# A one-core decoder layer on Trainium2: small tiles padded so that matmul operands start at the same place modulo 256 bytes

## The chip, the cores and the metric

The kernel runs on 1 core of one Trainium2 chip. The metric is the time of one execution in microseconds (us), as the device reports it; the figure used is the median of several runs. For the kernel before the change it is 2510.06 us (3 runs, 2508.91 to 2510.13).

## What is computed

One layer of a decoder trunk over 2048 tokens of width 1024, all in float32, with normalisation before and after each half. The first half mixes tokens by two head groups, a chunkwise mLSTM (4 heads) and a causal attention with compressed keys and values (8 heads); the second half is a feed-forward network of width 4096 with a squared ReLU.

```python
a = rmsnorm(x, norm_pre_mix[l])
mix = token_mixer(a, cos, sin, w_in[l], ...)   # [mLSTM || attention](a @ w_in) @ w_out
x = x + rmsnorm(mix, norm_post_mix[l])
m = rmsnorm(x, norm_pre_mlp[l])
y = jnp.square(jax.nn.relu(m @ w_up[l])) @ w_down[l]
x = x + rmsnorm(y, norm_post_mlp[l])
```

## The kernel before

Every large product is made of TensorE matmuls of fp32r tiles in three passes: each float32 operand is split into a high part, rounded to fp32r, and the rest, the low part, and the kernel adds high by high, high by low and low by high (the helper `mm3`, lines 198 to 200, and the same three lines written out in `up`, lines 2107 to 2109, and in `down`, 2339 to 2341). Nearly every one of these matmuls has 128 stationary columns (512 bytes of each partition) and 512 moving columns (2048 bytes of each partition). The splits are made by ScalarE (the high part, a cast) and VectorE or GpSimd (the subtraction).

The work has five stages; the times are of the profiled execution.

1. Input projection and mLSTM, 0 to about 490 us: `unit` (line 400) and `values` (832) multiply the weights `wh`, `wl` by the transposed input `xh`, `xl`; `chunk` (878) runs the recurrence.
2. Attention, to about 1040 us: `maxima` (1384) and `step` (1444) make scores `S` from `Kh`, `Kl` and `Qh`, `Ql`, then multiply the exponentials `ph`, `pl` by the values `V` (lines 1483 and 1486). `V` is one tile whose slices lie 129 numbers (516 bytes) apart.
3. Output projection, to about 1205 us: `group` (1714) multiplies `wo` by `hh`, `hl`, k tile by k tile (eight of them).
4. Up product, to about 1790 us: `up` (2092) makes seven products for each pair of column blocks (a Strassen scheme), 12 matmuls each.
5. Down product, to the end: `down` (2326), the same scheme with 6 matmuls a product, adds into the tiles `y` (`into`, line 2350), and `finish` (2399) normalises and stores.

The order on each engine is found beforehand by a small planner (`Plan`, with costs and due times given by hand) and then pinned. Transfers are issued by the SP queue in the planner's order.

SBUF tiles come from pools that are stacked from the left end and from the right end of each partition's bytes, a pool at a time (`sb`, line 202). A tile takes its bytes rounded up to a multiple of 32. Nearly all tiles are multiples of 256 bytes, so where a pool's tiles start modulo 256 is set by the few small ones that were placed before them: `mhalf` (line 228, 32 bytes), `col` (140 bytes), the row maxima `mx` (16 bytes, line 1423), the sums `rsm` (16 bytes, line 1570), `onecol` (260 bytes, line 1163), `gcol` (32 bytes, line 1678) and `v2` (64 bytes, line 2231).

Of the kernel before, what the change touches and what calls it, by code (L numbers as in the profile page):

```python
# [10 lines left out]
F32 = mybir.dt.float32  # L11
F32R = mybir.dt.float32r
# [6 lines left out]
P = 128  # L19
SEQ = 2048  # L20
DM = 1024
KD = DM // P
TB = 512
NB = SEQ // TB
NT = SEQ // P
# [164 lines left out]
def trunk(ctx: ExitStack, tc: tile.TileContext, x, xT, pos, wu, uqw, ukw, uvw, wout, wup, wdn, cols, rows, consts, edge, out, dbg=None):  # L190
# [3 lines left out]
    vec, act, pool, pe = nc.vector, nc.scalar, nc.gpsimd, nc.tensor  # L194
# [7 lines left out]
    def sb(stack, name, bufs, side="left"):  # L202
        return stack.enter_context(tc.tile_pool(name=name, bufs=bufs, side=side, reuse_waits="tile"))
# [17 lines left out]
    top = ctx.enter_context(tc.tile_pool(name="top", bufs=1))  # L221
# [3 lines left out]
    col = top.tile([P, C_N], F32, tag="col", name="col")  # L225
    ident = cst[:, K_ID : K_ID + P]
    maskT = cst[:, K_MASKT : K_MASKT + P]
    mhalf = top.tile([P, 8], F32, tag="mhalf", name="mhalf")
    identr = top.tile([P, P], F32R, tag="identr", name="identr")

    hT = dram.tile([DM, SEQ], F32, tag="hT", name="hT")
# [11 lines left out]
    pl = Plan()  # L243
    mark = len(nc.cur_bb.bb.instructions)
    s_b, s_x, s_e, pc, pa = (ExitStack() for _ in range(5))
    b1 = sb(s_b, "b1", 1, "right")
    b2 = sb(s_b, "b2", 2, "right")
    ps1 = pp(s_b, "ps1", 1, "right")
# [900 lines left out]
    def switch3():  # L1149

        nonlocal av, ar2, pS, po, V, maskb, identb, onecol
        s_b.close()
        av = sb(pa, "av", 1, "right")
        maskb = av.tile([P, P], BF16, tag="maskb", name="maskb")
        identb = av.tile([P, P], BF16, tag="identb", name="identb")
        act.copy(maskb, maskT)
        act.copy(identb, ident)
        ar2 = sb(pa, "ar2", 2, "right")
        pS = pp(pa, "pS", SB_, "right")
        po = pp(pa, "po", 1, "right")  # L1160

        V = av.tile([P, NT, 4, 129], F32R, tag="V", name="V")
        onecol = av.tile([P, 65], F32R, tag="onecol", name="onecol")
        set_tiles(av, 1)

    pl.group = "switch"
# [217 lines left out]
    def maxima(h, qb, keys):  # L1384
        s = h % 2
        mp = {}
        reds = []

        def piece(j, kb, key):
            n = TB if kb < qb else (j + 1) * P  # L1390
            t = {}

            def mm():
                if "t" not in mp:
                    mp["t"] = a2.tile([P, 4, 4], F32, tag="mp", name=f"mp{h}_{qb}", bufs=4)
                q0 = qb * TB + j * P
                t["p"] = ps = pm[0].tile([P, TB], F32, tag="m", name=f"m{h}_{qb}_{j}_{kb}")
                pe.matmul(ps[:, :n], Qh[s][0:96, q0 : q0 + P], Kh[s][0:96, kb * TB : kb * TB + n], start=True, stop=True)  # L1398

            def red():  # L1400
                ps = t["p"]
                if kb < qb:
                    vec.tensor_reduce(mp["t"][:, j, kb : kb + 1], ps, axis=AX.X, op=ALU.max)  # L1403
                else:
                    vec.tensor_tensor_reduce(
                        out=ps[:, :n], in0=ps[:, :n], in1=maskneg[:, 512 - n :], op0=ALU.add, op1=ALU.max, scale=1.0, scalar=NEG,
                        accum_out=mp["t"][:, j, kb : kb + 1],
                    )

            head = not reds  # L1410
            a = pl.op("PE", n / 2.4 + (56 if n == P else 15), mm, [o_q[h, qb][0], o_k[h, kb][0], o_kr[s, kb]], key, take=("m", "mp") if head else ("m",))
            if head:
                mp["op"] = a
            reds.append(pl.op("DVE", n / 0.96 + (148 if kb < qb else 285), red, [a, o_mask] if head else [a, o_mask, mp["op"]], key - 3, free=[("m", a)]))

        todo = [(j, kb) for j in range(4) for kb in range(qb + 1)]
        for (j, kb), key in zip(todo, keys):
            piece(j, kb, key)
        t = {}
        key = keys[-1] - 3  # L1420

        def top_():
            t["m"] = a2.tile([P, 4], F32R, tag="mx", name=f"mx{h}_{qb}")
            vec.tensor_reduce(t["m"], mp["t"][:, :, 0 : qb + 1], axis=AX.X, op=ALU.max)

        def rows_():
            t["p"] = (pq if QR == "q" else pm[0]).tile([P, TB], F32, tag=QR, name=f"mt{h}_{qb}")
            for j in range(4):
                pe.matmul(t["p"][0:1, j * P : (j + 1) * P], t["m"][:, j : j + 1], identr, start=True, stop=True)

        def put():
            act.activation(Qh[s][96:97, qb * TB : (qb + 1) * TB], t["p"][0:1], AF.Copy, scale=-1.0)

        a = pl.op("DVE", 80, top_, reds, key, take=("mx",), free=[("mp", mp["op"])])
        b = pl.op("PE", 4 * 75, rows_, [a, o_const[s]], key, take=(QR,), free=[("mx", a)])
        war = [o_sc[n] for n, (hh, q, _) in enumerate(blocks) if (hh, q) == (h - 2, qb)]
        o_m[h, qb] = pl.op("Activation", 585, put, [b] + war, key, free=[(QR, b)])
# [108 lines left out]
    def out_rows(h, qb, o_first, o_end, key):  # L1546
        t = {}
        end = (h, qb) == (NH - 1, NB - 1)
        bs = slice(qb * TB, (qb + 1) * TB)

        def copy():
            t["t"] = (pools["o1"] if end else ar2).tile([P, TB], F32, tag="ot", name=f"ot{h}_{qb}", bufs=1)
            act.copy(t["t"][0:64], acc_of[h, qb][0][64:128])

        def add0():
            vec.tensor_tensor(t["t"][0:64], t["t"][0:64], acc_of[h, qb][0][0:64], ALU.add)  # L1556

        def copy1():
            t["u"] = xrow("ou") if end else ar2.tile([P, TB], F32, tag="ou", name=f"ou{h}_{qb}", bufs=1)
            vec.tensor_copy(t["u"][0:65], acc_of[h, qb][1][0:65])  # L1560

        def both_():
            pool.tensor_tensor(t["t"][0:64], t["t"][0:64], t["u"][0:64], ALU.add)

        def store():
            dma(hT[512 + h * 64 : 576 + h * 64, bs], t["t"][0:64])
            dma(sumd[h : h + 1, bs], t["u"][64:65])

        def load():
            t["r"] = (pools["o1"] if end else ar2).tile([P, 4], F32, tag="rsm", name=f"rsm{h}_{qb}")  # L1570
            dma(t["r"], sumd[h, bs].rearrange("(p e) -> p e", e=4))

        def rec():
            vec.reciprocal(t["r"], t["r"])

        def put():
            dma(recd[h, bs].rearrange("(p e) -> p e", e=4), t["r"])

        o_ot = pl.op("Activation", 585, copy, [o_end], key - 3, take=() if end else ("ot",))
        z = pl.op("DVE", 680, add0, [o_ot], key - 3, free=[("o0", o_first)])  # L1580
        o_ou = pl.op("DVE", 680, copy1, [o_end], key - 3, take=("xr" if end else "ou",), free=[("o1", o_first)])
        if end:
            o_tail.extend((o_ot, o_ou))
            pl.group = "end"
        a = pl.op("Pool", 1260, both_, [z, o_ou], key - 3)
        b = pl.op("SP", 1000, store, [a], key - 3, free=[("xr", o_ou)] if end else [("ot", o_ot), ("ou", o_ou)], kb=130)
        c = pl.op("SP", 500, load, [b], key - 3, take=() if end else ("rsm",), kb=10)
        d = pl.op("DVE", 94, rec, [c], key - 3)
        o_out[h, qb] = b, pl.op("SP", 500, put, [d], key - 3, free=[] if end else [("rsm", c)], kb=10)
# [80 lines left out]
    def right():  # L1670
        pa.close()
        pools["xa"] = sb(ctx, "xa", 1, "right")
        pools["o3"] = sb(po2, "o3", 1, "right")
        pools["pmC"] = pp(pA, "pmC", 1)
        pools["ux"] = pp(ctx, "ux", 1, "right")
        pools["pmB"] = pp(po2, "pmB", 1, "right")
        pools["ss2"] = pools["xa"].tile([P, NT], F32, tag="ss2", name="ss2")
        pools["gcol"] = pools["xa"].tile([P, KD], F32, tag="gcol", name="gcol")
        pools["gpost"] = pools["o3"].tile([P, DM], F32, tag="gpost", name="gpost")
        dma(pools["gcol"], rows[:, R_PRE : R_PRE + DM].rearrange("o (k p) -> p (o k)", p=P))  # L1680
        dma(pools["gpost"], rows[:, R_POST : R_POST + DM].broadcast_to((P, DM)))
# [546 lines left out]
    def open_w():  # L2228
        pools["w2"] = sb(ctx, "w2", 1)
        pools["gpm"] = pools["w2"].tile([P, DM], F32, tag="gpm", name="gpm")  # L2230
        pools["v2"] = pools["w2"].tile([P, NT], F32, tag="v2", name="v2")
        dma(pools["gpm"], rows[:, R_POSTM : R_POSTM + DM].broadcast_to((P, DM)))

        vec.tensor_scalar(pools["v2"], pools["ss2"], 1.0 / DM, EPS, ALU.mult, ALU.add)
        vec.scalar_tensor_tensor(pools["v2"], pools["v2"], EPS, pools["v2"], ALU.mult, ALU.mult)
# [310 lines left out]
```

## Time and profile before

| | |
|---|---|
| median of 3 runs | 2510.06 us |
| the profiled execution, its own time | 2511.95 us |
| its span in the trace | 2510.2 us |
| TensorE (PE) busy | 2438.2 us, 97% of the span |
| weight loads (PEld) busy | 1940.5 us, 77% |
| VectorE (DVE) busy | 1811.9 us, 72% |
| ScalarE (ACT) busy | 1349.8 us, 54% |
| GpSimd (POOL) busy | 860.7 us, 34% |
| mean granted TensorE clock | 0.992 of full |

Times in the trace count from the span's start. A matmul's row in the time line gives its start and a modelled duration of about 0.39 us; successive matmuls overlap, so the time that a matmul costs in an uninterrupted stream is the distance from its start to the next one's start, here called the pace. Weight loads have rows of their own (PEld) and run beside the matmul ahead of them.

### The profile page before, as it was taken

What the parts mean: (1) busy time and instruction counts of PE and PEld (TensorE: products, weight loads), DVE (VectorE), ACT (ScalarE), POOL (GpSimd) and SP (SyncE); (2) the same over time, 40 slices, a digit from 0 to 9 for tenths busy, and PEclk for the clock granted to TensorE, in tenths of its full rate; (3) what the DMA queues carried; (4) which work ended last, traced back from release to release, by engine and by line L of the source; (5) the groups of instructions that cost most, each with busy time, mean ns of one, the idle gap of its engine ahead of it and who ended that gap; (6) DMA issues with size and microseconds to landing.
All of it is one profiled execution on the core that took longest, in us unless ns stands there. A gap on an engine that the chain in (4) does not pass through costs nothing.

```text
span 2510.2 us, 34019 instructions
## 1 busy us (share of the span) xinstructions
PE 2438.2 (97%) x11091; PEld 1940.5 (77%) x11091; DVE 1811.9 (72%) x3213; ACT 1349.8 (54%) x2625; POOL 860.7 (34%) x728
## 2 busy tenths in 40 slices
PE   8999999999999999899999999999999999999997
PEld 6778787777777777688888888888878878788875
DVE  5867667588878877645866688766675687776688
ACT  4535343366777777544666557655665343433343
POOL 3442423358998898422000000000000223233235
PEclk9999999999999999999999999999999999999998
DMA  6554544500000000567777698655674445444546
GB/s 214 154 166 144 171 158 143 149 19 15 17 20 11 16 14 15 170 213 242 251 220 214 196 307 260 198 172 160 178 231 145 141 133 170 128 143 157 180 162 231
DMA packets 308026, 378.14 MB, mean 151 GB/s; under 512 B 32028, under 2 KB 218408, under 8 KB 307656
## 3 DMA queue, kind: packets, MB, share of 16 engines
q1 hardware_dynamic: 304264, 368.58, 47.7%
q0 software_dynamic: 3584, 7.39, 1.1%
q8 instruction: 87, 1.43, 0.2%
q14 instruction: 91, 0.75, 0.1%
HBM read 251.93 MB, written 121.85 MB: 149 GB/s over the span
## 4 chain that ended last, share of the span: by engine, by line
PE 80%; DVE 9%; POOL 4%; issue 3%; DMA 2%; ACT 2%; SPq 0%; DVEq 0%; POOLq 0%; ACTq 0%
POOL t L1497 2%; PE m L1398 2%; PE mm L198 2%; PE S L198 2%; PE mm L199 2%; PE mm L200 2%; PE o L1483 2%; PE S L199 2%; PE S L200 2%; PE o L1486 2%; PE op L198 2%; PE op L200 2%; PE op L199 2%; DVE cy L806 1%; PE mv L199 1%
## 5 line engine op out<-in xcount | busy, mean ns | idle before, releaser
L2378 POOL TENSOR_TENSOR y<-vd_0X,y 128x512 f32<-128x512 f32 x6 | 9.7, 1615 | 738.2 <-ACT vd_0X L2375 719.4
L1462 ACT ACTIVATE ph<-S 128x512 fp32r<-128x512 f32 (+1 forms) x320 | 170.5, 533 | 94.9 <-PE S L200 47.1
L1497 POOL TENSOR_TENSOR t<-t,ph 128x512 f32<-128x512 f32 (+1 forms) x192 | 211.5, 1102 | 19.2 <-ACT ph L1462 8.7
L2289 ACT CAST hh<-hr 128x512 fp32r<-128x512 f32 (+1 forms) x192 | 106.5, 566 | 162.5 <-DMA hr<-hd 35.0
L1470 DVE TENSOR_TENSOR pl<-S,ph 128x512 fp32r<-128x512 f32 (+3 forms) x272 | 157.3, 590 | 35.0 <-ACT S L1466 31.2
L198 PE MATMUL mm<-xh,wh 128*128 128x512 f32 x384 | 158.4, 412 | 9.8 <-ACT xh L339 8.5
L1403 DVE TENSOR_REDUCE mp<-m 128x1 f32<-128x512 f32 x192 | 130.2, 684 | 33.5 <-PE m L1398 32.1
L2294 DVE TENSOR_TENSOR hl<-hr,hh 128x512 fp32r<-128x512 f32 (+1 forms) x192 | 129.3, 683 | 33.3 <-ACT hh L2289 23.6
L199 PE MATMUL mm<-xl,wh 128*128 128x512 f32 x384 | 152.0, 396 | 0.0
L200 PE MATMUL mm<-xh,wl 128*128 128x512 f32 x384 | 151.9, 396 | 0.0
L1466 ACT ACTIVATE S<-S 128x512 f32<-128x512 f32 (+3 forms) x272 | 141.1, 519 | 0.1
L198 PE MATMUL S<-Qh,Kh 97*128 97x512 f32 (+1 forms) x320 | 121.9, 381 | 1.6 <-DVE pl L1470 1.4
L1483 PE MATMUL o<-ph,V 128*128 128x512 f32 (+1 forms) x320 | 119.5, 374 | 0.5 <-DVE ot L1556 0.5
L1486 PE MATMUL o<-pl,V 128*65 128x512 f32 (+1 forms) x320 | 113.8, 364 | 4.9 <-DVE pl L1470 4.0
L199 PE MATMUL S<-Ql,Kh 97*128 97x512 f32 (+1 forms) x320 | 118.1, 369 | 0.0
L200 PE MATMUL S<-Qh,Kl 97*128 97x512 f32 (+1 forms) x320 | 117.8, 368 | 0.0
L373 ACT CAST wh<-wr 128x1024 fp32r<-128x1024 f32 (+1 forms) x65 | 66.7, 1032 | 91.0 <-PE mm L199 63.7
L1398 PE MATMUL m<-Kh,Qh 96*128 96x512 f32 (+2 forms) x320 | 111.8, 385 | 1.0 <-DVE mp L1403 0.6
L2128 ACT ACTIVATE t<-t 128x512 f32<-128x512 f32 x96 | 60.6, 631 | 83.4 <-DVE t L2123 82.9
L198 PE MATMUL op<-wo,hh 128*128 128x512 f32 x256 | 101.4, 396 | 0.6 <-DVE x L1798 0.6
L200 PE MATMUL op<-wo,hl 128*128 128x512 f32 x256 | 100.1, 391 | 0.0
L199 PE MATMUL op<-wo,hh 128*128 128x512 f32 x256 | 100.0, 391 | 0.0
(6432 smaller groups left out, 7779.8 us busy)
## 6 DMA issues: line engine op xcount, KB each, us to landing
hr<-hd SPq DMA_DIRECT2D x92, 448.0 KB
hd<-t SPq DMA_DIRECT2D x128, 256.0 KB
wr<-in_wu_dram SPq DMA_DIRECT2D x63, 512.0 KB
hd<-ts SPq DMA_DIRECT2D x96, 256.0 KB
xt<-in_x_dram SPq DMA_DIRECT2D x28, 512.0 KB
xf<-xd SPq DMA_DIRECT2D x40, 256.0 KB
hr<-hT SPq DMA_DIRECT2D x64, 128.0 KB
x1d<-x SPq DMA_DIRECT2D x16, 512.0 KB
```

Of the source, the lines that this page charges most:

```text
L198: pe.matmul(o, ah, bh, start=start, stop=False)
L199: pe.matmul(o, ah, bl, start=False, stop=False)
L200: pe.matmul(o, al, bh, start=False, stop=stop)
L1398: pe.matmul(ps[:, :n], Qh[s][0:96, q0 : q0 + P], Kh[s][0:96, kb * TB : kb * TB + n], start=True, stop=True)
L1403: vec.tensor_reduce(mp["t"][:, j, kb : kb + 1], ps, axis=AX.X, op=ALU.max)
L1462: act.activation(t["h"][:, :w], t["S"][:, :w], AF.Exp)
L1466: act.activation(t["p"][:, :w], t["S"][:, :w], AF.Exp)
L1470: (pool if by_pool else vec).tensor_tensor(t["l"][:, :w], t["p"][:, :w], f32(t["h"][:, :w]), ALU.subtract)
L1483: pe.matmul(o0, v[:, 0:128], t["h"][:, :w], start=start, stop=stop)
L1486: pe.matmul(o1, v[:, 64:129], t["l"][:, :w], start=start, stop=stop)
L1497: pool.tensor_tensor(to, to, hv, ALU.add)
L2294: vec.tensor_tensor(t["l", m][:, :w], t["r", m][:, :w], f32(t["h", m][:, :w]), ALU.subtract)
```

## The change

Some small tiles are made larger, and one tile that nothing reads, `edger` (96 bytes, at the right end), is added and filled once. The parts that the program uses keep their size: each padded tile is cut back to its old width where it is made.

```diff
-    mhalf = top.tile([P, 8], F32, tag="mhalf", name="mhalf")
+    mhalf = top.tile([P, 16], F32, tag="mhalf", name="mhalf")[:, 0:8]
...
+    edger = sb(ctx, "edger", 1, "right").tile([P, 24], F32, tag="edge", name="edger")
+    vec.memset(edger, 0.0)
...
-        onecol = av.tile([P, 65], F32R, tag="onecol", name="onecol")
+        onecol = av.tile([P, P], F32R, tag="onecol", name="onecol")[:, 0:65]
...
-            t["m"] = a2.tile([P, 4], F32R, tag="mx", name=f"mx{h}_{qb}")
+            t["m"] = a2.tile([P, 32], F32R, tag="mx", name=f"mx{h}_{qb}")[:, 0:4]
...
-            t["r"] = (pools["o1"] if end else ar2).tile([P, 4], F32, tag="rsm", name=f"rsm{h}_{qb}")
+            t["r"] = (pools["o1"].tile([P, 64], F32, tag="rsm", name=f"rsm{h}_{qb}") if end else ar2.tile([P, 32], F32, tag="rsm", name=f"rsm{h}_{qb}"))[:, 0:4]
...
-        pools["gcol"] = pools["xa"].tile([P, KD], F32, tag="gcol", name="gcol")
+        pools["gcol"] = pools["xa"].tile([P, 48], F32, tag="gcol", name="gcol")[:, 0:KD]
...
-        pools["v2"] = pools["w2"].tile([P, NT], F32, tag="v2", name="v2")
+        pools["v2"] = pools["w2"].tile([P, 64], F32, tag="v2", name="v2")[:, 0:NT]
```

The instructions and their order are the same on every engine but for one more MEMSET (of `edger`) at the head of VectorE's; one load of latent tiles for attention, issued by GpSimd, waits for one transfer fewer. What moves is where tiles start. The two built programs give the start of each operand; modulo 256 bytes, for the matmuls with 512 moving columns:

| products | matmuls | before: moving, stationary | after: moving, stationary |
|---|---|---|---|
| input projection, `unit` and `values` | 1536 | 128, 128 | 32, 32 |
| scores and maxima in attention | 896 | 160, 160 or 224, 224 | 128, 128 |
| keys | 96 | 160, 160 | 128, 128 |
| queries | 192 | 160, 96 | 128, 128 |
| `ph` and `pl` by `V` | 448 | 128, and 192 + a multiple of 4 | 128, and 128 + a multiple of 4 |
| output projection, k tiles 0 to 5 | 576 | 96, 96 | 128, 128 |
| output projection, k tiles 6 and 7 | 192 | 128, 96 | 128, 128 |
| up | 1536 | 224, 96 | 128, 128 |
| up | 864 | 128, 96 | 128, 128 |
| up | 288 | 96, 96 | 128, 128 |
| down | 1656 | 96, 128 | 128, 128 |
| down | 948 | 160, 128 | 128, 128 |
| down | 84 | 96 or 160, 224 | 128, 128 |

Below, a matmul whose two starts are equal modulo 256 is called even, another one uneven.

## Rows read from the trace of the kernel before

**Rows 1.** The page: engines' busy time, and PE and its clock in 40 slices.
```profile
span 2510.2 us, 34019 instructions
PE 2438.2 (97%) x11091; PEld 1940.5 (77%) x11091; DVE 1811.9 (72%) x3213; ACT 1349.8 (54%) x2625; POOL 860.7 (34%) x728
...
PEclk9999999999999999999999999999999999999998
```

**Rows 2.** Busy time by stretch: length, engines' busy us (instructions), clock, DMA share.
```profile
1040.00:1187.00 147.00, 145.95 (x670) 119.84 (x669) 75.73 (x126) 60.75 (x126) 37.87 (x25) 1.00 0.70 225
1187.00:1800.00 613.00, 613.00 (x2672) 495.76 (x2671) 436.27 (x685) 379.45 (x677) 4.55 (x5) 1.00 0.72 219
1800.00:2420.00 620.00, 617.85 (x2645) 495.51 (x2644) 445.46 (x665) 256.07 (x461) 142.72 (x99) 1.00 0.50 156
2420.00:2510.00 90.00, 69.54 (x275) 52.83 (x273) 75.51 (x120) 33.31 (x84) 47.21 (x41) 0.93 0.67 223
```

**Rows 3.** What PE waited for, 1040 to 2420: us in total, times, longest.
```profile
PE d_1X L2339 <- DVE y L2362: 1.3, 2, 0.7
PE op L198 <- DVE x L1798: 0.6, 1, 0.6
```

**Rows 4.** Time line of PE, output projection, k tiles 0 to 5.
```profile
1064.77 0.39 PE L198 MATMUL op<-wo,hh 128*128 128x512 f32 x1
...
1074.97 0.40 PE L198 MATMUL op<-wo,hh 128*128 128x512 f32 x1
```

**Rows 5.** Time line of PE, output projection, k tiles 6 and 7, from there on.
```profile
1075.21 0.39 PE L199 MATMUL op<-wo,hh 128*128 128x512 f32 x1
...
1080.58 0.40 PE L198 MATMUL op<-wo,hh 128*128 128x512 f32 x1
```

**Rows 6.** Time line of PE, input projection: an uninterrupted run of even matmuls.
```profile
413.69 0.39 PE L200 MATMUL mm<-xh,wl 128*128 128x512 f32 x1
...
423.89 0.39 PE L200 MATMUL mm<-xh,wl 128*128 128x512 f32 x1
```

**Rows 7.** Time line of PE, up product.
```profile
1600.17 0.40 PE L2108 MATMUL 1_2X<-x_61l,u 128*128 128x512 f32 x1
...
1699.83 0.39 PE L2107 MATMUL 1_8Y<-x_10h,u 128*128 128x512 f32 x1
```

**Rows 8.** Time line of PE, down product.
```profile
1900.16 0.40 PE L2340 MATMUL d_4X<-d,hh 128*128 128x512 f32 x1
...
1999.99 0.39 PE L2339 MATMUL d_7Y<-d,hh 128*128 128x512 f32 x1
```

**Rows 9.** Time line of PE, up product: even matmuls right after transposes.
```profile
1291.85 0.39 PE L2108 MATMUL 0_3X<-x_40l,u 128*128 128x512 f32 x1
...
1294.15 0.39 PE L2109 MATMUL 0_3X<-x_43h,u 128*128 128x512 f32 x1
```

**Rows 10.** Time line of PE in attention: two even score matmuls, two with `V`.
```profile
700.75 0.39 PE L199 MATMUL S<-Ql,Kh 97*128 97x512 f32 x1
700.98 0.39 PE L200 MATMUL S<-Qh,Kl 97*128 97x512 f32 x1
701.21 0.40 PE L1483 MATMUL o<-ph,V 128*128 128x512 f32 x1
701.45 0.39 PE L1486 MATMUL o<-pl,V 128*65 128x512 f32 x1
```

**Rows 11.** What PE waited for, 2420 to the end.
```profile
PE d_4Y L2339 <- DVE y L2362: 2.0, 1, 2.0
PE d_6Y L2339 <- DVE y L2362: 2.0, 1, 2.0
```

**Rows 12.** Time line of VectorE at the start.
```profile
1.19 0.06 DVE L290 MEMSET mrow<- 1x4 f32 x1
5.37 1.34 DVE L378 TENSOR_TENSOR wl<-wr,wh 128x512 fp32r<-128x512 f32 x2 [4.12 <-ACT wh L373]
```

**Rows 13.** Output projection by line: durations min/median/max, around 1078 and 1162 us.
```profile
L200 PEld LDWEIGHTS op<-wo,hl x7: 187/187/188, 1075.9 to 1080.1; 128*128 128x128 f32 x7
...
L200 PEld LDWEIGHTS op<-wo,hl x24: 187/188/188, 1154.3 to 1170.0; 128*128 128x128 f32 x24
```

**Rows 14.** VectorE's costliest group, 1187 to 2420: busy us, mean ns, idle before.
```profile
L2294 DVE TENSOR_TENSOR hl<-hr,hh 128x512 fp32r<-128x512 f32 (+1 forms) x168 | 112.5, 678 | 32.3 <-ACT hh L2289 22.6 <-PE d_2X L2340 3.3 <-PE d_3X L2340 2.1
```

## The prediction

> **What bounds the kernel now.** I read the page first, then the busy time by stretch, the list of what TensorE waited for, and last the time line of TensorE, in which the start of each matmul stands. The page shows TensorE busy for 97% of the span at an almost full clock [rows 1]. A busy share alone says little, since successive matmuls overlap, so the stages have to be looked at one by one. From 1187 to 1800 us, the up product, TensorE is busy without a gap; from 1800 to 2420, the down product, it misses 2.2 of 620 us, both at a granted clock of 1.00, the 2.4 GHz level [rows 2]. In all of 1040 to 2420 its waits have six entries that come to 2.7 us, of which the two longest are shown [rows 3]. So over these 1380 us the time is the number of matmuls times the pace at which they follow each other, and nothing else ends last. Only the last 90 us differ: TensorE is busy for 69.5 of them and VectorE for 75.5 [rows 2], and TensorE waits for VectorE's additions to `y` [rows 11].
>
> The pace is not one number. In the output projection the same source lines, the same shapes and the same accumulation go through the k tiles one after the other. Over k tiles 0 to 5 the rows from 1064.77 to 1074.97 are 46 starts, 45 distances in 10.20 us: 226.7 ns [rows 4]. The next 24 distances, to 1080.58, take 5.61 us: 233.8 ns [rows 4, 5]. Between the two stretches only the place of `wo` changes: up to there both operands start at 96 modulo 256 bytes, from there the moving one starts at 128 and the stationary one still at 96. No wait falls between them. The input projection, whose operands both start at 128, runs at the first pace again: 46 starts from 413.69 to 423.89, 226.7 ns [rows 6]. The up product, mostly uneven, makes 428 distances in 99.66 us: 232.9 ns [rows 7]. The down product, all of it uneven, makes 428 in 99.83 us: 233.3 ns [rows 8]. So I take it that an uneven matmul costs about 6 ns more than an even one, at any of the unequal residues that occur here, and that equality counts, not the residue itself (96 and 128 give the same 226.7).
>
> A rule of the Trainium skill speaks against this. TensorE: Matmul & The Clock Gate, Part 2, "Step-by-step: what each phase is for", says that TensorE has two independent read ports into SBUF, one for the moving operand and one for the weights, and that loading the next weights takes no bandwidth from the running matmul. By that rule the placement could not matter and the sum would be zero; the trace disagrees with it by the step from 226.7 to 233.8 ns. The weight loads' own rows do not tell the two cases apart (187 ns either way [rows 13]), so their durations can't be used to judge it.
>
> **The change, part by part.**
>
> *Up.* All 2688 matmuls become even. I take 227.0 ns as their new pace: 226.7 and a little for disturbances. After a pause or a few small matmuls, even ones too run slower for a while: eleven even up matmuls right after transposes make 10 distances in 2.30 us, 230.0 ns [rows 9]. Such pauses are rare in this stage. 2688 x (232.9 - 227.0) = 15.9 us.
>
> *Down.* 2688 matmuls become even. Some 275 stand in the last 90 us [rows 2]; there TensorE waits for VectorE, and I count their gain as nothing. 2413 x (233.3 - 227.0) = 15.2 us. The cover lost would be 275 x 6.3 = 1.7 us more, an end of the range.
>
> *Output projection.* 192 matmuls, 192 x (233.8 - 227.0) = 1.3 us.
>
> *Attention.* The score matmuls are even already and yet follow at 230 ns, and the two with `V` at 230 to 240 [rows 10]: runs of two or three matmuls between narrower ones never settle. Making them even in another place does nothing by this, and `V`, with slices 516 bytes apart, stays uneven. I take zero. The best end is the settled pace for all of its 1632 matmuls with 512 columns, from 233: 1632 x 6 = 9.8 us. An end below zero comes from nothing here that I see.
>
> *Input projection.* From 128, 128 to 32, 32: even before and after, zero (but see the third rival).
>
> *The rest.* The MEMSET of `edger` stands before the first work of VectorE that waits for data: its short MEMSETs take 0.06 us [rows 12], and VectorE then stands idle until 5.37 us. That idle time covers it; without the cover it would cost 0.1 us. The wait that one load loses costs nothing. Other engines keep their work and order, and only need to keep up: VectorE is busy for 436 of 613 us in up and 445 of 620 in down [rows 2], which a TensorE 2.6% faster raises from 72% to 74%. The DMA share rises from 0.72 to 0.74.
>
> The sum is 15.9 + 15.2 + 1.3 = 32.4 us. The profiled execution took 2511.95 us (a span of 2510.2 and 1.75 around it), so it would take 2479.6. It stands 1.9 us above the median of the runs, 2510.06, and the same sum from the median gives 2477.7; I predict **2478 us**.
>
> Bounds of this case. Best: 226.7 throughout (5293 x 0.3 = 1.6 us), the tail (1.7) and attention (9.8) come in: 2465. Worst: the MLP never settles and keeps the 230.0 ns of [rows 9]: 2688 x 2.9 + 2413 x 3.3 + 1.3 = 17.1 us, 2493.
>
> **The rivals.**
>
> *Partial gain.* The even pace in up and down stays at the disturbed 230.0 ns, because something in the MLP disturbs the stream all the time. For it: those are the only even matmuls within the MLP. Against it: they stand right behind transposes, and the uneven streams of the MLP run without a pause. It gives 2493 us.
>
> *The residue counts, not the equality.* If 32 is a bad place where 96 and 128 are good ones, the 1536 matmuls of the input projection lose 6 ns each, 9.2 us, and the result is 2487. Against it: two different residues already give the same pace [rows 4, 6].
>
> *The change doesn't do what it says, or the pace is set by something else* that changes with the tile, so that nothing moves: 2510 us. Here the rule of the two ports would come true. Against it stands the step within one accumulation [rows 4, 5].
>
> *Slower.* The new places could slow VectorE's reads in the down product, and then VectorE would become its bound. It decides only when VectorE's 445 us of work exceed the 605 that TensorE would need, that is, when its operations take 36% longer, 920 instead of 678 ns for the group `hl` [rows 14]. The stage would then go like the last 90 us, where 275 matmuls take 327 ns each and the clock is 0.93 [rows 2]: 2413 x 94 ns, well over 200 us more; just past the deciding point, at 45% longer, VectorE needs 645 us and the kernel takes 2510 + 25 - 17 = 2518. Nothing in the trace speaks for it: VectorE's operands are read at the unequal and the equal places already.
>
> **How the numbers follow.** Forecast 0.80, partial gain 0.10, the residue 0.04, nothing 0.04, slower 0.02. What this kernel's measurements can tell from no change is 0.2%, 5 us. The first three cases are faster by more, so faster 0.94, same 0.04, slower 0.02. The range runs from 2470 to 2490: the forecast with some of attention's gain at one end, and at the other the residue and about half way to the partial gain. What it leaves out is half of that rival, the last two, and the extreme ends of the forecast, under 2 in 10.
>
> **What would show it.** In the profile after: up and down at 227 ns between starts, over 400 distances, with no new waits of TensorE; the up stage near 597 us in place of 613 and the down stage near 605 in place of 620; k tiles 6 and 7 of the output projection at the pace of the others; input projection and attention as long as before. It would be wrong if even matmuls in the MLP kept 230 ns or more, if the input projection fell to 233, or if TensorE's waits from 1187 to 2420 grew to several us.

## The result and the profile after

The median after is 2485.43 us (6 runs, 2481.76 to 2491.66), beside 2510.62 us for the kernel before on the same chip (6 runs, 2508.91 to 2513.03): a ratio of 0.9903, with a 95% interval of 0.9889 to 0.9916, so 25 us or 1.0% faster. The profiled execution took 2481.76 us, the shortest of its six; that of before, 2511.95 us, stood 1.3 us above its median. So the two traces differ by 30.2 us, 5 more than the medians. Of all the executions in this document two, one of the kernel before and one of `ctl256` below, ran at a granted clock of about 0.65 and took 3452 and 3685 us; the ratios leave them out.

The busy time by stretch answers to [rows 2] (length, busy us and count of each engine, clock, DMA share, GB/s; the lines of the code stand three further down than before):

```profile
1187.00:1790.00 603.00, 601.27 (x2681) 496.80 (x2681) 436.33 (x687) 379.58 (x676) 2.79 (x4) 1.00 0.75 223
1790.00:2400.00 610.00, 605.26 (x2647) 496.55 (x2646) 450.89 (x674) 258.66 (x468) 153.62 (x105) 1.00 0.51 160
2400.00:2480.00 80.00, 61.20 (x245) 47.26 (x244) 67.04 (x107) 27.72 (x70) 40.51 (x35) 0.92 0.68 224
```

As many instructions now take 603 us where they took 613, and 610 where they took 620. What is new is in the second number: TensorE, without a gap in the up product before, now misses 1.7 of 603 us, and in the down product 4.7 in place of 2.2.

These rows are cut at round times, and the first is not the up stage alone: in before the first of the 2688 up matmuls starts at 1221 us and the last at 1857, and the row from 1187 also holds 148 matmuls of the output projection. Followed matmul by matmul, the matmuls that took 613.1 us in before, from 1187 to 1800, take 601.1 after, those that took 619.9, from 1800 to 2420, take 605.0, and the last 273, which took 79.6, take 79.8.

The pace is read from the time line of TensorE. In the output projection, across all eight k tiles without a step (79 distances in 17.91 us, 226.7 ns):

```profile
1064.00 0.39 PE L200 MATMUL op<-wo,hl 128*128 128x512 f32 x1
...
1081.91 0.39 PE L198 MATMUL op<-wo,hh 128*128 128x512 f32 x1
```

In the up product, 177 distances in 40.12 us, and in the down product 177 in 40.12 us, both 226.7 ns:

```profile
1599.81 0.39 PE L2110 MATMUL 1_3X<-x_41h,u 128*128 128x512 f32 x1
...
1639.93 0.39 PE L2110 MATMUL 1_6X<-x_00h,u 128*128 128x512 f32 x1
...
1949.75 0.39 PE L2344 MATMUL d_4X<-d,hl 128*128 128x512 f32 x1
...
1989.87 0.39 PE L2344 MATMUL d_7X<-d,hl 128*128 128x512 f32 x1
```

To see what each stage gave, all distances from one matmul's start to the next instruction's start were summed from the two traces. "Mean" is over the distances under 250 ns; "long" is what longer ones take beyond 227 ns (waits, pauses, stretches at the lower clock).

| stage | sum before, us | mean before, ns | long, us | sum after | mean after | long |
|---|---|---|---|---|---|---|
| up (2688) | 627.0 | 232.68 | 1.6 | 614.1 | 226.99 | 4.0 |
| down (2687) | 646.0 | 233.04 | 20.1 | 632.6 | 226.92 | 22.9 |
| output projection (768) | 178.4 | 228.98 | 2.5 | 177.2 | 227.39 | 2.5 |
| scores, 512 columns (672) | 162.9 | 232.35 | 7.1 | 163.4 | 232.12 | 7.7 |
| queries (192) | 46.7 | 231.39 | 2.3 | 46.4 | 230.62 | 2.2 |
| input projection, `mm` (1152) | 281.5 | 228.22 | 18.7 | 283.4 | 228.17 | 20.7 |

The waits of TensorE that are new or longer, in up and then in down (us in total, times, longest):

```profile
PE 0_13X L2110 <- ACT tu L2122: 1.4, 1, 1.4
PE 0_12X L2110 <- DVE t L2126: 0.4, 1, 0.4
...
PE d_2X L2344 <- DVE hl L2297: 2.1, 3, 1.6
PE d_0X L2342 <- DVE y L2365: 1.1, 2, 0.5
```

The wait of 1.59 us for `hl` is not new: in before it stood 31 us later, behind 2420. It fell into the last 90 us there and into the down row here, so that the missing time of the down row grew by less than it seems to.

### The profile page after: what moved, and what is told of

The parts are those of the page before. It is cut to its first block, busy times and chain, and to the rows that moved or that the text cites. A ratio compares the mean times of both kernels' runs of the same rounds, so it can differ in the third digit from the quotient of the medians.

```text
span 2480.1 us, 34020 instructions
## 1 busy us (share of the span) xinstructions
PE 2409.3 (97%) x11091; PEld 1940.9 (78%) x11091; DVE 1808.1 (73%) x3214; ACT 1349.9 (54%) x2625; POOL 863.6 (35%) x728
## 4 chain that ended last, share of the span: by engine, by line
PE 80%; DVE 9%; DMA 3%; POOL 3%; ACT 2%; issue 2%; SPq 1%; DVEq 0%; POOLq 0%; ACTq 0%
PE mm L198 2%; PE mm L199 2%; PE mm L200 2%; PE S L198 2%; PE m L1401 2%; PE o L1486 2%; PE op L198 2%; PE op L199 2%; PE S L199 2%; PE op L200 2%; PE S L200 2%; PE o L1489 2%; POOL t L1500 1%; DVE cy L809 1%; DVE y L2365 1%
## 5 line engine op out<-in xcount | busy, mean ns | idle before, releaser
L1406 DVE TENSOR_REDUCE mp<-m 128x1 f32<-128x512 f32 x192 | 130.1, 684 | 31.4 <-PE m L1401 30.2
```

## The experiments

Throughout, the distance is the start of the moving operand minus that of the stationary one, modulo 256 bytes; even is 0. Two rivals to "equality of the two residues sets the pace" had to go first: that the extra tile or the new places as such do something, and that the padding helps by another way than the matmuls' operands.

**The change once more, and a shift by 256 bytes.** `again` is the changed kernel unaltered. `ctl256` is the kernel before with one added tile of 256 bytes at the right end, so every tile there moves and no residue does:

```diff
+    edger = sb(ctx, "edger", 1, "right").tile([P, 64], F32, tag="edge", name="edger")
+    vec.memset(edger, 0.0)
```

> The changed kernel once more. The pace alone (up and down at 227 ns in place of 233) is worth 31 to 32 us, the profiled execution showed 30 of them, the median of its runs only 25. Theory 1 (the even starts set the pace, and what the median lacks is the clock of single executions): median 2480 to 2486, up and down at 226.9 to 227.1 ns on average again, and executions that take longer show a lower granted clock, about 0.988 where the shorter ones show 0.990. Theory 2 (the change itself makes TensorE wait more, and the clock falls after those waits): all executions stay at 2485 or above, with waits of TensorE in up and down over 10 us.

> The kernel before, with one tile of 256 bytes and its MEMSET at the right end: everything on the right moves by 256 bytes, so no matmul changes between even and uneven. Theory 1 (equality modulo 256): no change, 2508 to 2514, up and down at 233.0 ns. Rival (the equality counts at a larger step, such as 512, or any shift of the tiles changes the time): a different pace in up and down, by 1 ns or more, and a time off by 5 us or more. Its executions also show how far the granted clock of a kernel with the old pace varies.

`again`: 2484.39 us against 2511.12, 0.9893 [0.9879, 0.9906], with paces of 226.97 and 226.89 ns. `ctl256`: 2510.10, 0.9998 [0.9988, 1.0007], with 232.67 and 233.06. Moving the tiles does nothing while the residues stay. Of what was expected of `again`, the time and the pace came out, but the clock sorts its four executions only in part: 2480.53 and 2486.46 us had 0.992 and 0.988, yet 2482.75 had 0.989 and 2486.04 had 0.991. Why the median of the first runs gained 25 us where its trace shows 30 stays open.

**All padding kept, the distance made 128.** One number of the changed kernel differs; 2400 of the 2688 matmuls in up and all of down become uneven by 128, while the padding, the MEMSET and the output projection stay as in the change:

```diff
-    edger = sb(ctx, "edger", 1, "right").tile([P, 24], F32, tag="edge", name="edger")
+    edger = sb(ctx, "edger", 1, "right").tile([P, 56], F32, tag="edge", name="edger")
```

> The changed kernel with the tile at the right end larger by 128 bytes: up (2400 of 2688) and down (all) become uneven by 128, all other matmuls stay even. Theory 1: up and down fall back to 232.7 to 233.4 ns, and the time to 2508 to 2514, as before. Rival (starts need to be equal modulo 128 only, or the small tiles act in some other way): 227 ns stay, 2480 to 2488.

Measured: 2509.51 us, 0.9994 [0.9985, 1.0003]; the means are 232.65 in up and 232.69 in down. The time line in up has 173 distances in 40.29 us, 232.9 ns:

```profile
1599.67 0.39 PE L2111 MATMUL 1_2X<-x_61l,u 128*128 128x512 f32 x1
...
1639.96 0.40 PE L2110 MATMUL 1_4X<-x_63h,u 128*128 128x512 f32 x1
```

128 more bytes in a tile that nothing reads take the whole gain back. The rule that the prediction weighed, two independent read ports (Trainium skill, TensorE: Matmul & The Clock Gate, Part 2, "Step-by-step: what each phase is for"), would by that reading have had this kernel and the changed one equal. They lie 25 us apart, and the measurement decides.

**Distances of 64 in either sign.** With 160 bytes in `edger` the distance is -64 in up's 2400 matmuls and +64 in down; with 32 bytes the signs are exchanged.

```diff
-    edger = sb(ctx, "edger", 1, "right").tile([P, 24], F32, tag="edge", name="edger")
+    edger = sb(ctx, "edger", 1, "right").tile([P, 40], F32, tag="edge", name="edger")
```

> As the kernel that is uneven by 128, but by 64: in the trace of before only the queries in attention were uneven by 64, in runs too short to tell. Theory 1 in its strict form (any unequal start costs 6 ns): 232 to 233.5 ns in up and down, 2506 to 2514. Weaker form (the cost grows with the distance): a pace between 227 and 233, about 230, and 2493 to 2500. Rival (equal modulo 64 is enough): 227 ns, 2480 to 2488.

`d64`: 2501.07 us, 0.9962 [0.9948, 0.9975]. Up stays at 232.9 ns (172 distances in 40.05 us), but down runs at 228.9 (176 in 40.28):

```profile
1599.75 0.39 PE L2110 MATMUL 1_2X<-x_62h,u 128*128 128x512 f32 x1
...
1639.80 0.39 PE L2111 MATMUL 1_4X<-x_63l,u 128*128 128x512 f32 x1
...
1899.69 0.39 PE L2343 MATMUL d_5Y<-d,hh 128*128 128x512 f32 x1
...
1939.97 0.39 PE L2342 MATMUL d_0X<-d,hh 128*128 128x512 f32 x1
```

"Unequal costs 6 ns" is thus too simple. Either the sign matters or the stage does; `dm64`, with `[P, 8]` in the same place, tells these apart.

> The change with 32 bytes in place of 96 in edger. The distance moving - stationary becomes +64 in 2400 of the 2688 up matmuls and -64 in all of down: the signs of the kernel with 160 bytes, exchanged. Theory: the size and sign of the distance modulo 256 set the pace, so up (its 2400) runs at 229.0 ns and down at 233 ns; against the change up loses 2400 x 2.0 = 5 us and down 2688 x 6 = 16, some 2504 us. Rival: the stage decides (its operands, its accumulation, what the other engines do), and the sign does not: then up stays at 232.9 and down at 229.0, some 2501 us with the loss in up.

`dm64`: 2501.28 us against 2510.34, 0.9967 [0.9954, 0.998]. Now up is the quicker one, 175 distances in 40.11 us, 229.2 ns, and down has 172 in 40.13, 233.3:

```profile
1599.69 0.39 PE L2111 MATMUL 1_3Z<-x_21l,u 128*128 128x512 f32 x1
...
1639.80 0.39 PE L2112 MATMUL 1_5Z<-x_23h,u 128*128 128x512 f32 x1
...
1899.65 0.40 PE L2342 MATMUL d_6X<-d,hh 128*128 128x512 f32 x1
...
1939.78 0.40 PE L2343 MATMUL d_2X<-d,hh 128*128 128x512 f32 x1
```

At a distance of 64 the sign decides and not the stage: +64 costs about 2 ns, -64 about 6. The time is 3 us under the 2504 expected, for TensorE waits less in the slower down product: its long distances come to 17.4 us, against 22.9 in after.

**One of the paddings undone.** Without the padding of `gcol`, 864 matmuls in up lie at distance 160 and nearly all of down at 96:

```diff
-        pools["gcol"] = pools["xa"].tile([P, 48], F32, tag="gcol", name="gcol")[:, 0:KD]
+        pools["gcol"] = pools["xa"].tile([P, KD], F32, tag="gcol", name="gcol")
```

> The changed kernel without one of its paddings, that of gcol: what lies behind it on the right moves by 160 bytes. 864 matmuls of up (moving start minus stationary start 160 modulo 256) and 2604 of down (96) become uneven, 1824 of up and all others stay even. Theory 1: the even ones of up stay at 227, the others go to 229 to 234, so a mean of 228 to 229.5 in up and 229 to 234 in down, and a time 8 to 22 us over the changed kernel's, by how many are uneven and not by which stage. Rival (the tiles' absolute places, or one padding alone, carry the gain): up and down move together, or neither moves.

Measured: 2503.02 us, 0.9976 [0.9966, 0.9986]. Up has a mean of 229.53 ns (1824 of its matmuls are even), down 233.18. Matched one by one with the starts in the built program, the even matmuls of up have a mean of 227.6 ns and those at distance 160 one of 233.6. The pace goes by the single matmul: a stage that is two thirds even keeps part of the gain.

**Attention made uneven.** The score and maxima matmuls (896) were even before and after. A gap of 128 bytes between the tiles of K and Q makes them uneven; 672 of them are the scores of 512 columns.

```diff
+            if n == "Kl":
+                gap = pool_.tile([P, 32], F32, tag=f"gap{s}", name=f"gap{s}")
+                vec.memset(gap, 0.0)
```

> The changed kernel with a tile of 128 bytes between the keys and the queries: all 896 score and maxima matmuls with 512 columns in attention become uneven by 128, nothing else does; two MEMSETs are added. Theory 1 (short runs never settle, so evenness is worth nothing there): scores at 231 to 233 ns as before, same time within 3 us. Rival (attention profits too and would lose it): 2 to 6 ns more for each, 2 to 5 us, if TensorE is what attention waits for.

Measured: 2484.21 us, 0.9898 [0.9883, 0.9913], no change from the changed kernel (`again`, on another chip, 2484.39; `again2`, on the same chip, 2485.31). The mean distance of the scores is 233.04 ns; in after it is 232.12, and in the other kernels with even scores 231.8 to 232.4. In attention, where runs of two or three matmuls stand between narrower ones, evenness is worth 1 ns a matmul, some 1 us in all, too little to be seen in the time.

**Sixteen bytes.** The tiles of `u` and `d` are cut out of one large tile, 16 bytes past an even place; up then has a distance of -16, and down and the output projection's k tiles 0 to 5 one of +16.

```diff
-        return pools[where].tile([P, 2, TB], F32R, tag=ring, name=name, bufs=4 if ring == "wx" else 1)
+        if where == "o1":
+            return pools[where].tile([P, 2, TB], F32R, tag=ring, name=name, bufs=4)
+        k = int(ring[1:])
+        i, count = (k, WB) if where == "work" else (k - WB, W2B)
...
+        lo = 4 + i * 2 * TB
+        return pools[big][:, lo : lo + 2 * TB].rearrange("p (a b) -> p a b", a=2)
```

> The changed kernel with the weights' tiles of output projection (k tiles 0 to 5), up and down carved out of one large tile, 16 bytes past their even place: moving minus stationary is 240 (minus 16) in up, 16 in down and in 576 of the output projection. Theory 1 in its strict form (any unequal start costs): up and down at 229 to 234 ns, 2492 to 2512. Rival (only lines of 32 bytes or more count): 226.9 stays, as the changed kernel. A third possibility, after the 229.0 that down showed at 64: some small distance is better than none, and one of the stages falls below 226.7.

Not settled. Ten executions took 2492.62, then 2498.06 to 2498.91 (three), then 2505.87 to 2508.35 (six); the median is 2506.77, and the ratio, 0.9967 [0.995, 0.9984], stands for none of the three groups. In the profiled one, 2498.91 us, down ran at 231.7 ns (173 distances in 40.08 us), and most of up at the even pace, 178 in 40.35 us, 226.7 ns:

```profile
1599.62 0.39 PE L2119 MATMUL 1_2X<-x_63l,bigwork 128*128 128x512 f32 x1
...
1639.97 0.39 PE L2120 MATMUL 1_5Y<-x_12h,bigwork 128*128 128x512 f32 x1
...
1899.69 0.39 PE L2350 MATMUL d_5X<-bigwork,hh 128*128 128x512 f32 x1
...
1939.77 0.40 PE L2352 MATMUL d_1X<-bigwork,hl 128*128 128x512 f32 x1
```

But up had two paces at one and the same distance. From 1282 to 1433 us its stream is cut by groups of four transposes into 15 stretches; 4 of them ran at 226.7 ns and 11, with 376 matmuls, at 233.0 to 233.8, and the pace changed at the transposes alone. Here 64 distances in 14.51 us, 226.7 ns, stand ahead of such a group, and 51 in 11.90 us, 233.3 ns, behind it, both at a granted clock of 1.00:

```profile
1296.00 0.39 PE L2118 MATMUL 0_3X<-x_50h,bigwork 128*128 128x512 f32 x1
...
1310.51 0.39 PE L2119 MATMUL 0_4Y<-x_33l,bigwork 128*128 128x512 f32 x1
...
1310.97 0.60 PE L1860 MATMUL xtr<-cst,xl 128*128 128x128 f32 x4
...
1311.88 0.40 PE L2120 MATMUL 0_4X<-x_40h,bigwork 128*128 128x512 f32 x1
...
1323.78 0.39 PE L2120 MATMUL 0_5Y<-x_11h,bigwork 128*128 128x512 f32 x1
```

So at -16 a stretch runs at one of two paces, and what picks it was not found. An estimate from these numbers: had the 1502 matmuls that follow each other from 1499 us on come out at 233.3 ns, this execution would have been 1502 x 6.6 = 9.9 us longer, 2508.8, near the six slower ones. No trace of a slower one shows it, and that of 2492.62 us stays unexplained. That a small distance is safe can't be taken from this run.

**The planner told the new pace.** The planner lays out the other engines' work by a figure of 695 ns for three matmuls; at 227 ns they take 681.

```diff
-            last = products(nm, s, i, [(kk,) for kk in range(4)], passes, t, af, key + 2.5 * i, fr, 695)
+            last = products(nm, s, i, [(kk,) for kk in range(4)], passes, t, af, key + 2.5 * i, fr, 681)
...
-            return products(nm, s, j, [(e,) for e in range(2)], passes, t, af, key + 1.2 * j, fr, 695)
+            return products(nm, s, j, [(e,) for e in range(2)], passes, t, af, key + 1.2 * j, fr, 681)
```

> The changed kernel with the planner told the new pace: 681 in place of 695 ns for three matmuls of up and down. Only the order on the engines changes, a little. TensorE waited 1.8 us in up and some 13 in down and its end. If the planner's old costs make the new waits: 2 to 5 us less than the changed kernel. If not: the same within 3 us, either way.

> The change as it is, once more, beside replan2 on the same chip: 2484 us if the executions before it stand, up and down at 227.0 ns, the waits of up's first half (1.4 and 0.4 us) in the profiled execution again.

> The change with the planner's figure for three matmuls at 681 ns in place of 695 in up and down, once more beside the change itself on the same chip. Theory: with the true pace the work of the other engines is laid out closer to where it is due, the waits of the change shrink by 1 to 2 us, and it is 1 to 3 us faster than again2. Rival: the order hardly differs, the difference seen so far (2482 against 2484 us) is the scatter between executions, and both medians lie within 1 us.

`replan`: 2482.17 us, 0.9889 [0.9874, 0.9904]. On one chip, against 2510.34 us before: `again2` 2485.31 (four runs, 2484.39 to 2485.98), 0.9898 [0.9882, 0.9913]; `replan2` 2481.00 (four, 2479.95 to 2483.63), 0.9882 [0.9867, 0.9898]. The four runs of one lie below the four of the other, so 681 is very likely some 4 us faster, more than expected, though the intervals of the two ratios overlap. But the reason expected is wrong: the sums of up are alike (612.6 us in `again2`, 614.2 in `replan2`, and the 1.4 us wait is missing in both). Between these two traces the difference is in down, 633.0 against 629.2. The same three rows of TensorE's time line stand here of before, of after and of `replan2`; in `replan2` the matmuls of `d_2X` and `d_2Y` follow each other without the wait for `hl`. First before:

```profile
2426.21 0.50 PE L2341 MATMUL d_2X<-d,hl 128*128 128x512 f32 x1 [1.60 <-DVE hl L2294]
2426.55 0.39 PE L2339 MATMUL d_2Y<-d,hh 128*128 128x512 f32 x1
...
2427.94 0.39 PE L2339 MATMUL d_1X<-d,hh 128*128 128x512 f32 x1
```

The same matmuls in after:

```profile
2395.00 0.80 PE L2344 MATMUL d_2X<-d,hl 128*128 128x512 f32 x1 [1.59 <-DVE hl L2297]
2395.59 0.63 PE L2342 MATMUL d_2Y<-d,hh 128*128 128x512 f32 x1
...
2398.15 0.44 PE L2342 MATMUL d_1X<-d,hh 128*128 128x512 f32 x1
```

And in `replan2`:

```profile
2393.78 0.39 PE L2344 MATMUL d_2X<-d,hl 128*128 128x512 f32 x1
2394.01 0.39 PE L2342 MATMUL d_2Y<-d,hh 128*128 128x512 f32 x1
...
2395.37 0.39 PE L2342 MATMUL d_1X<-d,hh 128*128 128x512 f32 x1
```

The six matmuls behind the wait take 1.39 us in before, 2.56 in after and 1.36 in `replan2`. In after they run at the lower clock level: from 2390 to 2400 us the granted clock is 0.83, in `replan2` 1.00 (the number ahead of the DMA share). The row of after:

```profile
2390.00:2400.00 10.00, 7.70 (x26) 5.67 (x25) 9.02 (x14) 4.46 (x11) 6.39 (x6) 0.83 0.60 197
```

The row of `replan2`:

```profile
2390.00:2400.00 10.00, 8.25 (x37) 6.51 (x35) 9.03 (x16) 5.35 (x13) 7.24 (x6) 1.00 0.64 220
```

So the same wait of 1.6 us costs 1.2 us more in after, for the clock falls behind it, which it did not do in before (1.00 from 2420 to 2430 there). `again`, `again2` and `unevenS`, with the figure of 695, have the wait and the fall as after has them (0.91 from 2385 to 2405 us in each of the four); both `replan` traces have neither, and in exchange a longer wait for `y` at 2400 us, 1.83 in place of 0.68. This accounts for some 2 us; the remaining 2 of the difference are not assigned.

One trace of each does not settle it, though. `unevenS`, with the figure of 695, has the wait and the fall, and its down comes to 629.2 us all the same. Behind 2405 us it has the waits that after has, but its clock falls less, 0.98 against 0.92, and its last 240 matmuls take 64.9 us against 68.0. First after, then `unevenS`:

```profile
2405.00:2478.00 73.00, 56.89 (x228) 44.03 (x226) 62.99 (x101) 26.11 (x67) 39.08 (x34) 0.92 0.68 224
2405.00:2478.00 73.00, 57.76 (x244) 44.68 (x242) 67.41 (x107) 27.43 (x70) 40.62 (x35) 0.98 0.71 237
```

So the clock of the last 75 us can be worth 3 us with nothing changed in the order of the down product, and where the 4 us of the new figure come from stays open. Why the clock falls in after and not in before was not tried.

## Why the prediction was right, point by point

The forecast was 2478 us, in a range of 2470 to 2490, faster. The median is inside the range and 7 us above the forecast. The mechanism is the forecast one; some of the size was not.

*Up, 15.9 us.* The pace fell from 232.68 to 226.99 ns, and 2688 x 5.69 = 15.3 us is what it gave; the other 0.6 lies in the pace of before, 232.7 over the stage and 232.9 in the stretch that was read. The stage gained 12.9, since its long distances grew from 1.6 to 4.0 us. This is the first mis-sized piece: the term had 227.0 for everything and no new wait, though the text named the growth of the waits as a thing to watch. In the profiled execution the largest new wait stands at 1488 us:

```profile
1488.32 0.62 ACT L2055 CAST u<-u_15r 128x512 fp32r<-128x512 f32 x1 [1.40 <-DMA u_15r<-in_wup_dram]
1488.85 0.58 ACT L2122 COPY tu<-0_13X 128x512 f32<-128x512 f32 x1
...
1489.48 0.50 PE L2110 MATMUL 0_13X<-x_50h,u 128*128 128x512 f32 x1 [1.36 <-ACT tu L2122]
```

ScalarE waits for the load of `u_15r`, and its copy `tu`, which frees what TensorE writes next, is queued behind that cast. The DMA engines had little room here already: their share is 0.96 in these 50 us, and was 0.95 in the corresponding stretch of before.

```profile
1450.00:1500.00 50.00, 48.27 (x211) 39.07 (x210) 41.17 (x65) 31.10 (x56) 0.00 (x0) 1.00 0.96 304
```

The prediction looked at the share of the whole stage, 0.72, which hides this stretch. In before ScalarE waited as long for the same load (1.37 us), and TensorE had no gap. The gap returned in `again`, not in `again2`: there up's only wait is one of 0.7 us. In `replan2` the same stretch has a share of 0.97 and no gap. So a full DMA makes the wait possible and does not force it; that it is the cause was argued from these rows and not tried by taking transfers away.

*Down, 15.2 us.* The stage as a whole, the last 90 us included, gained 13.4. The pace gave 2687 x (233.04 - 226.92) = 16.4 us, which takes in the tail's matmuls; the long distances took 2.8 back (20.1 to 22.9). Two parts of that are seen: waits for `y` of 0.3 to 0.5 us ahead of 2400, and the clock behind the wait for `hl`. "Counted as nothing" for the last 275 matmuls was right: 273 of them took 79.6 us before and 79.8 after.

*Output projection, 1.3 us.* 1.2 measured (the pace of 233.8 ns came from rounded starts and is 233.5). *Attention and input projection, 0.* The scores went from 232.35 to 232.12 ns, the input projection from 228.22 to 228.17; `unevenS` shows by itself that the whole of the scores' evenness is worth 1 us. The long distances of the input projection lie between 18.4 us (`dm64`) and 22.8 (`replan2`) in kernels that do not differ in that stage, so its 2 us more are scatter.

Together the three terms measured 12.9 + 13.4 + 1.2 = 27.5 us in place of 32.4. From the median of before, 2510.6, that is 2483.1; the executions of the change scatter over 10 us around 2485.4, and the other 2.3 us are within that.

*The rivals.* Partial gain: no, the pace in the MLP is 227.0 on the mean and not 230. The residue: no, 32, 32 in the input projection runs as 128, 128 did. Nothing moves: no, and `d128` against `again` shows that the placement alone does it. Slower by VectorE: its group `hl` keeps its median of 678 ns (the mean goes from 678 to 701), and VectorE is busy for 450.9 of 610 us in down.

*The signs that were named.* Over the same instructions up came out at 601.1 us where 597 was named, down at 605.0 where 605 was. TensorE's waits did grow: from 1187 us to the end of the down row it misses 6.5 us in place of 2.2, and 4.2 without the waits of 0.7 and 1.6 us for `hh` and `hl`, which stood behind 2420 in before. That is 2 of the forecast 32 us, and a mild form of the sign against it.

*"At any of the unequal residues"* was the weak sentence. It holds for the output projection, up and down of the kernel before, and fails for +64. The period is 256: the shift by 256 changed nothing, and the even matmuls of after, of which 864 in up and 1668 in down have operands an odd multiple of 256 bytes apart in the built program, run at the same 226.7 ns.

## What to carry to other kernels

Where a long stream of matmuls is the whole of a stage's time, read the distance between starts and not the busy share; where it differs between stages of the same shape, compare where the moving and the stationary operand start modulo 256 bytes in SBUF. Here, on one core, with fp32r tiles and a weight load for every matmul, equality was worth 2.5% of such a stage, for some padding of small tiles that nothing reads, and next to nothing in a stage of short runs. Aim at equal places and not at a small distance: at -16 the same program ran at either pace. When the stream gets faster, look for the fullest stretch of the DMA rather than its mean, and tell a planner the new pace, though the gain of that was measured here and not explained.

## What was not expected of the hardware

The cost is not symmetric and does not grow with the distance. With fp32r tiles, 128 stationary and 512 moving columns the pace is 226.7 ns at a distance of 0, 228.9 to 229.2 at +64, 231.7 at +16, 232.7 to 232.9 at 128 and 232.9 to 233.3 at -64. In before it is 233.0 at -32 and 233.1 to 233.3 at +32, and in `nogcol` 233.3 at +96 and 233.6 at -96, as means over all the matmuls of a stage at that distance. At -16 it was 226.7 or 233.3, stretch by stretch. At 0 no stretch of up or down stayed at an upper pace in the six traces that have all of both stages even: past the first nine matmuls of a stretch, no nine successive ones had a mean over 231 ns. What in the chip makes it so was not found: the trace shows starts, and not the reads of SBUF.
